# SiLU's tables kept loaded through the first projection, norms two blocks behind, and left-hand buffers 32 bytes lower

## The chip, the cores and the metric

The kernel runs on one core of one Trainium2 chip. The metric is device time in microseconds of one execution, lower is better; the times shown are medians of several runs. TensorE (PE) multiplies, with its weight loads shown as PEld; VectorE (DVE), ScalarE (ACT) and GpSimd (POOL) do the elementwise work and the gathers; SyncE (SP) issues most transfers.

## What is computed

One inference step of a one-layer encoder on 1024 prompt frames and 32 sample frames of width 1024. The part that matters here is the projection of the normalised input and the short convolution behind it:

```python
h = rms_norm(x, norm_mix_w)
proj = h @ w_in
gq, gk, gv, glr, gg, dqkv, da, db, dz = _split_cols(proj, IN_SIZES)
conv = conv_in[:, 0:l] * gdn_conv_w[0]
for i in range(1, CONV_W):
    conv = conv + conv_in[:, i:i + l] * gdn_conv_w[i]
conv = jax.nn.silu(conv)
cq, ck, cv = _split_cols(conv, (GDN_QK, GDN_QK, GDN_V))
q2 = l2_norm(cq.reshape(b, l, GDN_HEADS, GDN_DK)) * (GDN_DK ** -0.5)
k2 = l2_norm(ck.reshape(b, l, GDN_HEADS, GDN_DK))
o1 = rms_norm(o1, gla_norm_w) * jax.nn.silu(gg).reshape(b, l, GLA_HEADS, GLA_DV)
o2 = rms_norm(o2, gdn_norm_w) * jax.nn.silu(dz).reshape(b, l, GDN_HEADS, GDN_DV)
```

Two recurrent mixers (GLA and gated delta, `gla` and `gdn_free`/`gdn_state`) follow, then an output projection, a retrieval over 16384 experts (PEER: keys, top 16, gathered rows of `u` and `v`), and a final norm.

## The kernel before

Tokens are tiled by 128 (tiles 0 to 7, and "S" of 32 sample frames). `project(g)` handles three groups of tiles, PROJ; group 0 is tiles 0, 1 and S. For each group it normalises and transposes the tiles into `hh` and `hl` (a high and a low part of each number, so that three matmuls make one product), then goes through three kinds of blocks of weight columns, each weight chunk `w` being loaded by SP and split into `wh` (ACT, L191) and `wl` (DVE, L192):

- one block for gates (`win_s`) and sixteen blocks `u` by channel (`win_c`): 24 matmuls of 288 columns into `pcm` (L324);
- blocks u = 4 to 15 are the convolution's: ACT copies `pcm` to `ci`, scales it into `row` (L393), DVE adds three shifted products (L395), ACT applies SiLU in place (L397), and for the first eight of them squares `row` into `sq` (L401). `norms()` then sums the squares over channels with `pn` matmuls of one column (L364), and ACT copies `pn` to `ssn` (L366). After the eighth, `frame_norms` takes Ln and Exp of `ssn`;
- six blocks `u` by token (`win_t`) into `ptm` (L419), copied or put through SiLU into `o` (L427).

ACT holds one set of function tables at a time. SiLU is in another set than Ln and Exp, while Copy, Square and the casts run under either. `mixer_tables()` (L102) loads, at its place in the program, the set that has both Ln and Exp; where an instruction's set is not loaded, the build puts a load in front of it, under the line of that instruction.

Buffers come from pools that grow from the left (const, `sl`, `rt`, `mc`, `mx`, `p1`, later `da`) or from the right of SBUF (`gs`, `sp`, `ge`, `gp`, `dn`, `gx`, `dv`). The small `const` tiles lie in front of all other left pools, so their size shifts those.

The order of each engine's instructions is made when the kernel is built: the Tile scheduler goes through the program with a model of the engines' time and takes what is ready, by the order of the code. An edit in one place thus shifts choices far behind it. Each engine executes its own list strictly in order. After project(0), the mixers of one tile at a time are woven with the later projections (up to about 0.7 ms), then come the output projection and the routing, the gathers of expert rows `ug` and `vg` by POOL with their products on DVE and PE, and the dense half over all experts for tiles 2 to 5, `activations` (matmuls into `pD`, weights `uh`/`ul` from the pool `da`, moving `hh`/`hl` from `dn`) and `dense` (matmuls into `pV`, both operands from `dv`).

Of the kernel before, what the change touches and what calls it, by code (L numbers as in the profile page):

```python
# [11 lines left out]
F32 = mybir.dt.float32  # L12
# [3 lines left out]
U16 = mybir.dt.uint16  # L16
BF16 = mybir.dt.bfloat16
AF = mybir.ActivationFunctionType
ALU = mybir.AluOpType
AX = mybir.AxisListType  # L20

P = 128
# [10 lines left out]
OFFS = [0, 16, 24, 29, 33, 36, 38, 40, 42, 43, 44, 45, 46, 47, 48, 49]  # L33
# [36 lines left out]
def bc(ap, shape):  # L70
    return ap.to_broadcast(shape)
# [3 lines left out]
def layer_kernel(ctx: ExitStack, tc: tile.TileContext, A: dict):  # L75
    nc = tc.nc
    mm = nc.tensor.matmul

    const = ctx.enter_context(tc.tile_pool(name="const", bufs=1))
# [6 lines left out]
    rt = rctx.enter_context(tc.tile_pool(name="rt", bufs=1))  # L86
# [13 lines left out]
    def mixer_tables():  # L100

        tc.keep_in_program_order(nc.scalar.preload_act_table_set("natural_log_exp_and_others"))  # L102
# [18 lines left out]
    nc.gpsimd.iota(iota128, pattern=[[1, P]], base=0, channel_multiplier=0,  # L121
                   allow_small_or_imprecise_dtypes=True)

    offs = const.tile([P, 15], F32, name="offs")
    for q in range(15):
        nc.gpsimd.memset(offs[:, q:q + 1], float(OFFS[q + 1]))
    firsts = const.tile([P, 16], U16, name="firsts")
    for q in range(16):
        nc.gpsimd.memset(firsts[:, q:q + 1], OFFS[q] * P)

    noffs = const.tile([P, 15], F32, name="noffs")
    nc.vector.tensor_scalar(noffs, offs, -1.0, 1.0, op0=ALU.mult, op1=ALU.add)

    def row_bcast(name, src, n, pool):
        t = pool.tile([P, n], F32, name=name)
# [3 lines left out]
    def ntok(t):  # L139
        return DEC if t == "S" else P  # L140
# [126 lines left out]
    def project(g):  # L267
# [4 lines left out]
        first, last = g == 0, g == len(PROJ) - 1  # L272
# [4 lines left out]
        def pbank(name):  # L277
            turn[0] += 1
            return bank(name, streams[turn[0] % len(streams)])
# [12 lines left out]
        def chunk(src):  # L292
            w = rt.tile(list(src.shape), F32, name="w", tag="wqb", bufs=4)
            nc.sync.dma_start(w, src)
            wh = p1.tile(list(src.shape), F32R, name="wh", tag="wh", bufs=WB)
            wl = p1.tile(list(src.shape), F32R, name="wl", tag="wl", bufs=WB)
            return split(wh, wl, w)
# [20 lines left out]
        def by_channel(src):  # L318
            p = pbank("pcm")
            for kh in range(2):  # L320
                w = chunk(src[kh])
                for a, b in ((w[0], hh), (w[0], hl), (w[1], hh)):
                    for k in range(4):
                        mm(p[:, :N], a[:, k], b[:, kh * 4 + k, :N], start=b is hh and a is w[0] and kh + k == 0,  # L324
                           stop=a is w[1] and kh * 4 + k == KB - 1)
            return p

        def row_tile():
            return p1.tile([P, 3 * P], F32, name="row", bufs=2)
# [27 lines left out]
        sqs = []  # L357

        def norms():
            b, sq = sqs.pop(0)  # L360
            pn = bank("pn", "rt")
            for i, t in enumerate(tiles):
                n, o = ntok(t), i * P + (3 if t == "S" else 0)
                mm(pn[:n, i:i + 1], sq[:, o:o + n], ones[:, 0:1], start=True, stop=True)  # L364
            for i0, i1, n in pieces(g):
                nc.scalar.copy(ss[:n, i0:i1, b], pn[:n, i0:i1])  # L366
            if b == 7:
                frame_norms(g, p1, ss, ib)

        for u in range(16):  # L370
            p = by_channel(A["win_c"][u])
            if len(sqs) > (0 if u < 12 else -1) and sqs:
                norms()
            if u < 4:
                row = row_tile()
                nc.scalar.activation(row[:, :N], p[:, :N], AF.Copy, scale=0.125 if u < 2 else 1.0)
                nc.sync.dma_start(d_qk[g][:, u, :], row[:, :N])
                yield None
                continue
            b = u - 4  # L380

            nf = N - DEC if sample else N
            L = N + 3 if sample else N
            ci = p1.tile([P, 3 * P + 3], F32, name="ci", bufs=1)
            nc.vector.tensor_copy(ci[:, 0:3], hist[:, b, :])
            nc.scalar.copy(ci[:, 3:3 + nf], p[:, :nf])
            nc.vector.tensor_copy(hist[:, b, :], ci[:, nf:nf + 3])
            if sample:
                nc.vector.tensor_copy(ci[:, nf + 3:nf + 6], tails[:, b, :])
                nc.scalar.copy(ci[:, nf + 6:L + 3], p[:, nf:N])  # L390
                nc.vector.tensor_copy(tails[:, b, :], ci[:, L:L + 3])
            row = row_tile()
            nc.scalar.activation(row[:, :L], ci[:, 0:L], AF.Copy, scale=cw[:, b, 0:1])  # L393
            for i in range(1, 4):
                nc.vector.scalar_tensor_tensor(row[:, :L], ci[:, i:i + L], cw[:, b, i:i + 1], row[:, :L],  # L395
                                               op0=ALU.mult, op1=ALU.add)
            nc.scalar.activation(row[:, :L], row[:, :L], AF.Silu)  # L397
            mixer_tables()
            if b < 8:
                sq = p1.tile([P, 3 * P], F32, name="sq", bufs=1)  # L400
                nc.scalar.activation(sq[:, :L], row[:, :L], AF.Square)  # L401
                sqs.append((b, sq))
            nc.sync.dma_start(d_cv[g][:, b, 0:nf], row[:, 0:nf])
            if sample:
                nc.sync.dma_start(d_cv[g][:, b, nf:], row[:, nf + 3:L])
            yield None
        for u in range(6):
            c, hf = divmod(u, 2)
            acc = [pbank("ptm") for _ in range((ni + 1) // 2)]
            ps = [acc[i // 2][:, (i % 2) * 256:(i % 2) * 256 + 256] for i in range(ni)]  # L410
            for kh in range(4):
                w = chunk(A["win_t"][u, kh])
                for ws, hs in ((w[0], (hh, hl)), (w[1], (hh,))):
                    for i, t in enumerate(tiles):
                        n = ntok(t)
                        for k in range(2):
                            for h in hs:

                                mm(ps[i][:n], h[:, kh * 2 + k, i * P:i * P + n], ws[:, k],  # L419
                                   start=kh == 0 and k == 0 and ws is w[0] and h is hh and i % 2 == 0,  # L420
                                   stop=ws is w[1] and kh * 2 + k == KB - 1, skip_group_check=True)
                yield None
            os = []
            for i, t in enumerate(tiles):
                n = ntok(t)
                o = p1.tile([P, 256], F32, name="o", bufs=OB)
                nc.scalar.activation(o[:n], ps[i][:n], AF.Silu if c else AF.Copy)  # L427
                os.append(o)
            if c:
                mixer_tables()  # L430
            for i, (t, o) in enumerate(zip(tiles, os)):
                n = ntok(t)
                if c:
                    o3 = o[:n].rearrange("p (h e) -> p h e", h=2)
                    nc.vector.tensor_tensor(o3, o3, bc(gw[:n, c - 1, None, :], [n, 2, P]), op=ALU.mult)
                nc.sync.dma_start(d_tm[g][c, i * P:i * P + n, hf * 256:(hf + 1) * 256], o[:n])
            yield None
# [755 lines left out]
    p1 = p1ctx.enter_context(tc.tile_pool(name="p1", bufs=1))  # L1193
    spctx = ExitStack()
    sp = spctx.enter_context(tc.tile_pool(name="sp", bufs=1, side="right"))
    weave(project(0))


# [35 lines left out]
    sel, picked, mixT = {}, {}, {}  # L1234
    c1, c2, c3, chose = {}, {}, {}, [None]
    gdn_pending = {}
    behind, chosen = iter(()), []
    coming = {k: project(g) for g, ks in COMING.items() for k in ks[:1]}
    for g, ks in COMING.items():
        for k in ks[1:]:  # L1240
# [121 lines left out]
```

## Time and profile before

| | us |
|---|---|
| median of 3 runs (3272.29 to 3275.75) | 3274.96 |
| the profiled execution | 3281.99 |
| its span, first to last instruction | 3280.3 |
| PE busy in the span | 3064.6 (93%) |
| DVE busy | 2291.9 (70%) |
| ACT busy | 1282.0 (39%) |
| POOL busy | 1316.8 (40%) |

The page gives each engine's busy time, cuts the span into 40 slices with the granted TensorE clock of each, and follows the chain of work that ended last. Busy shares are means over stages with different limits, so the stages have to be read one by one: the first projection (to about 190 us), mixers and later projections (to about 700 us), routing and gathers (to about 1700 us), the dense half (to about 3200 us) and a short tail.

### The profile page before, as it was taken

The numbers are of one execution on the slowest core, as the hardware profiler recorded it, in microseconds if no ns is written. First come the engines' busy times: TensorE is split into PE (matmuls) and PEld (weight loads), VectorE is DVE, ScalarE is ACT, GpSimd is POOL, SyncE is SP. The second block draws the span as 40 slices with busy tenths as digits, with TensorE's granted clock in tenths as the row PEclk, the third lists the DMA queues.
The fourth block names the chain that finished last, engine by engine and source line by source line (L and its number), as shares of the span: only waits on it lengthen the run. The fifth ranks groups of instructions, "written<-read, shape, count | busy, mean of one in ns | idle before, by whom it ended". The sixth has DMA issues, their size and how long they took to land.

```text
span 3280.3 us, 49506 instructions
## 1 busy us (share of the span) xinstructions
PE 3064.6 (93%) x17739; PEld 2451.9 (75%) x17739; DVE 2291.9 (70%) x5692; ACT 1282.0 (39%) x2748; POOL 1316.8 (40%) x1181
## 2 busy tenths in 40 slices
PE   6999997799999999889789999999999999999997
PEld 6889986689878877767567777777777777776664
DVE  4457478888878989899977767766766767434332
ACT  6758434544332226787523222223222222223111
POOL 2100004433244544433355545544555555233454
PEclk9989998799999989899799999999999999999998
DMA  5532468888788889999999889889998898777988
GB/s 155 167 108 90 155 195 299 271 296 294 272 309 317 310 322 348 314 345 334 328 351 333 336 319 363 329 324 356 334 337 346 300 366 312 281 258 258 339 320 301
DMA packets 363977, 959.04 MB, mean 292 GB/s; under 512 B 35746, under 2 KB 137523, under 8 KB 359635
## 3 DMA queue, kind: packets, MB, share of 16 engines
q0 software_dynamic: 156672, 570.49, 47.5%
q1 hardware_dynamic: 141266, 351.84, 30.5%
q10 hardware_dynamic: 65792, 33.56, 3.5%
q8 instruction: 139, 2.28, 0.3%
q14 instruction: 108, 0.88, 0.1%
HBM read 893.00 MB, written 62.76 MB: 291 GB/s over the span
## 4 chain that ended last, share of the span: by engine, by line
PE 47%; DMA 1%; issue 1%; DVE 1%; POOL 0%; ACT 0%; POOLq 0%; DVEq 0%; ACTq 0%
PE pD L198 7%; PE pD L197 7%; PE pD L199 7%; PE pV L197 7%; PE pV L199 7%; PE pV L198 7%; PE pv L1139 6%; DMA vg<-v,eiT 1%; DMA ug<-u,ei 0%; POOL ug L1098 0%; DVE ug L1099 0%; DVE c L887 0%; DVE vl L192 0%; POOL ug L1133 0%; DVE xf L1052 0%
## 5 line engine op out<-in xcount | busy, mean ns | idle before, releaser
L1098 POOL DMA_INDIRECT ug<-u,ei x544 | 647.2, 1190 | 1148.8 <-DVE ug L1099 514.0
L1133 POOL DMA_INDIRECT vg<-v,eiT x488 | 582.9, 1194 | 625.8 <-PE pv L1139 453.2
L1099 DVE SCALAR_TENSOR_TENSOR ug<-ug,h 128x1024 f32<-128x1024 f32 x544 | 659.9, 1220 | 106.4 <-DMA ug<-u,ei 104.0
L197 PE MATMUL pD<-hh,uh 128*128 128x512 f32 x1024 | 408.6, 399 | 4.3 <-ACT uh L191 4.2
L198 PE MATMUL pD<-hh,ul 128*128 128x512 f32 x1024 | 408.6, 399 | 3.3 <-DVE ul L192 3.3
L199 PE MATMUL pD<-hl,uh 128*128 128x512 f32 x1024 | 407.4, 398 | 0.0
L198 PE MATMUL pV<-vh,wl 128*128 128x512 f32 x1024 | 401.4, 393 | 0.0
L199 PE MATMUL pV<-vl,wh 128*128 128x512 f32 x1024 | 400.0, 393 | 0.0
L197 PE MATMUL pV<-vh,wh 128*128 128x512 f32 x1024 | 381.5, 395 | 5.0 <-DVE acc L1039 4.3
L1039 DVE TENSOR_TENSOR acc<-acc,pV 128x512 f32<-128x512 f32 x248 | 164.0, 684 | 239.1 <-PE pV L199 213.0
L191 ACT CAST vh<-vx 128x1024 fp32r<-128x1024 f32 x128 | 129.2, 1047 | 509.9 <-PE pV L198 420.0
L991 ACT ACTIVATE w<-pD 128x512 f32<-128x512 f32 x128 | 76.5, 598 | 541.0 <-PE pD L199 482.3
L1139 PE MATMUL pv<-vg,wd 128*32 128x512 f32 x1952 | 267.6, 619 | 17.2 <-DMA vg<-v,eiT 16.4
L192 DVE TENSOR_TENSOR wl<-w,wh 128x512 fp32r<-128x512 f32 x302 | 207.3, 688 | 100.5 <-ACT wh L191 70.3
L191 ACT CAST wh<-w 128x512 fp32r<-128x512 f32 x302 | 186.0, 619 | 185.1 <-PE pcm L324 61.7
L534 PE MATMUL pq<-h2T,wqb 128*128 128x256 f32 (+2 forms) x1280 | 249.0, 348 | 3.5 <-ACT sc L556 2.0
L197 PEld LDWEIGHTS pD<-hh,uh 128*128 128x128 f32 x1024 | 193.4, 189 | 65.6 <-issue 14.1
L197 PEld LDWEIGHTS pV<-vh,wh 128*128 128x128 f32 x1024 | 192.3, 188 | 66.9 <-issue 14.2
L198 PEld LDWEIGHTS pD<-hh,ul 128*128 128x128 f32 x1024 | 193.3, 189 | 64.9 <-issue 12.2
L199 PEld LDWEIGHTS pD<-hl,uh 128*128 128x128 f32 x1024 | 193.2, 189 | 56.7 <-issue 11.7
L199 PEld LDWEIGHTS pV<-vl,wh 128*128 128x128 f32 x1024 | 192.7, 188 | 55.1 <-issue 14.3
L534 PEld LDWEIGHTS pq<-h2T,wqb 128*128 128x128 f32 x1280 | 211.2, 194 | 25.9 <-issue 3.0
(334 smaller groups left out, 5457.9 us busy)
## 6 DMA issues: line engine op xcount, KB each, us to landing
ux<-ut SPq DMA_DIRECT2D x128, 512.0 KB
vx<-v SPq DMA_DIRECT2D x128, 512.0 KB
wqb<-wq SPq DMA_DIRECT2D x80, 576.0 KB
gd<-gst ACTq DMA_DIRECT2D x16, 2048.0 KB
G<-gd SPq DMA_DIRECT2D x32, 1024.0 KB
w<-win_c SPq DMA_DIRECT2D x96, 256.0 KB
wch<-wout SPq DMA_DIRECT2D x40, 512.0 KB
w<-win_t SPq DMA_DIRECT2D x72, 256.0 KB
```

Source lines behind the costliest of these rows:

```text
L191: nc.scalar.copy(hi, x)
L192: nc.vector.tensor_tensor(lo, x, hi.bitcast(F32), op=ALU.subtract)
L197: mm(out, a[0], b[0], start=first, stop=False, **kw)
L198: mm(out, a[1], b[0], start=False, stop=False, **kw)
L199: mm(out, a[0], b[1], start=False, stop=last, **kw)
L534: mm(p[:, :N], w[:, kb, :], h2T[:, kb, :], start=(kb == 0), stop=(kb == KB - 1))
L991: nc.scalar.activation(w, pD, AF.Gelu_apprx_tanh)
L1039: nc.vector.tensor_tensor(acc[ti][:, cs], before[:, cs], p, op=ALU.add)
L1098: nc.gpsimd.indirect_dma_start(out=g, out_offset=None, in_=A["u"], in_offset=idx_of(ei[:, k:k + 1]))
L1099: nc.vector.scalar_tensor_tensor(g, g, 1.0, h2, op0=ALU.mult, op1=ALU.mult, accum_out=act[:, k:k + 1])
L1133: nc.gpsimd.indirect_dma_start(out=g, out_offset=None, in_=A["v"], in_offset=idx_of(eiT[:, tok:tok + 1]))
L1139: return mm(pv[half][c * 32:(c + 1) * 32, :], wd[:, c, :], vs[c][:, half * 512:(half + 1) * 512], start=(r == 0), stop=(r == ns - 1), tile ...
```

## The change

Four edits. (1) In the first projection `mixer_tables()` no longer follows each SiLU; it is called once, after the last block by token. (2) `norms()` there runs two blocks behind the squares as long as convolution blocks that square are being made, and the last two are taken one per block; `sq` of that projection comes from three buffers of the pool `rt` (tag `mixT`) and not from one of `p1`. (3) `noffs` is written by POOL directly, and `offs` and the DVE instruction that made `noffs` from it are gone. (4) `offs` took 64 bytes of each partition; `firsts` is allocated at twice its size, so that all left pools behind `const` start 32 bytes lower. Line numbers of the old kernel from L133 to L397 are three lower in the new one.

```diff
-    offs = const.tile([P, 15], F32, name="offs")
-    for q in range(15):
-        nc.gpsimd.memset(offs[:, q:q + 1], float(OFFS[q + 1]))
-    firsts = const.tile([P, 16], U16, name="firsts")
+    firsts = const.tile([P, 32], U16, name="firsts")[:, :16]
     for q in range(16):
         nc.gpsimd.memset(firsts[:, q:q + 1], OFFS[q] * P)
-
     noffs = const.tile([P, 15], F32, name="noffs")
-    nc.vector.tensor_scalar(noffs, offs, -1.0, 1.0, op0=ALU.mult, op1=ALU.add)
+    for q in range(15):
+        nc.gpsimd.memset(noffs[:, q:q + 1], float(1 - OFFS[q + 1]))
...
         for u in range(16):
             p = by_channel(A["win_c"][u])
-            if len(sqs) > (0 if u < 12 else -1) and sqs:
+            if len(sqs) > (1 if first and u < 12 else 0):
                 norms()
...
             nc.scalar.activation(row[:, :L], row[:, :L], AF.Silu)
-            mixer_tables()
+
+            if not first:
+                mixer_tables()
             if b < 8:
-                sq = p1.tile([P, 3 * P], F32, name="sq", bufs=1)
+                sq = (rt.tile([P, 3 * P], F32, name="sq", tag="mixT", bufs=3) if first else
+                      p1.tile([P, 3 * P], F32, name="sq", bufs=1))
...
-            if c:
+            if c and (u == 5 or not first):
                 mixer_tables()
```

What the scheduler made of it, at three places. PE, third to fifth convolution block of project(0), before (`pcm_836` is the next block by channel, `pn` the column sums of the squares `sq`):

```order
L324 MATMUL pcm_775<-hh_168,wl_797 128x288 x4
L364 MATMUL pn_690<-ones_84,sq_649 128x1 x2
L364 MATMUL pn_690<-ones_84,sq_649 32x1
L364 MATMUL pn_751<-ones_84,sq_710 128x1 x2
L364 MATMUL pn_751<-ones_84,sq_710 32x1
L364 MATMUL pn_812<-ones_84,sq_771 128x1 x2
L364 MATMUL pn_812<-ones_84,sq_771 32x1
L324 MATMUL pcm_836<-hh_168,wh_839 128x288 x4
```

and after:

```order
L321 MATMUL pcm_762<-hh_166,wl_766 128x288 x4
L321 MATMUL pcm_762<-hh_166,wh_783 128x288 x4
L321 MATMUL pcm_762<-hl_167,wh_783 128x288 x4
L361 MATMUL pn_739<-ones_84,sq_638 128x1 x2
L361 MATMUL pn_739<-ones_84,sq_638 32x1
L321 MATMUL pcm_762<-hh_166,wl_784 128x288 x4
L361 MATMUL pn_799<-ones_84,sq_698 128x1 x2
L361 MATMUL pn_799<-ones_84,sq_698 32x1
L321 MATMUL pcm_822<-hh_166,wh_825 128x288 x4
```

Three sums stood in a row with no block's matmuls between them; now each has some ahead of it, and nine groups of them stand behind the last of these. ACT over one of these blocks, before:

```order
L397 ACT_TABLE_LOAD
L397 ACTIVATE row<-row 128x291
L102 ACT_TABLE_LOAD
L386 COPY ci<-pcm 128x256
L390 COPY ci<-pcm 128x32
L401 ACTIVATE sq<-row 128x291
L393 ACTIVATE row<-ci,cw 128x291
L366 COPY ssn<-pn 128x2
L366 COPY ssn<-pn 32x1
```

and after:

```order
L394 ACTIVATE row<-row 128x291
L383 COPY ci<-pcm 128x256
L387 COPY ci<-pcm 128x32
L401 ACTIVATE sq<-row 128x291
L390 ACTIVATE row<-ci,cw 128x291
L188 CAST wh<-w 128x512 x2
L363 COPY ssn<-pn 128x2
L363 COPY ssn<-pn 32x1
```

The two loads are gone, and the two casts of the next weight chunks stand inside the block. The third place is on ACT where the first projection ends and the second begins (`ss` are the second's norms, `dec`, `G` and `kd` belong to the first tile's mixers), after the change:

```order
L302 ACT_TABLE_LOAD
L302 ACTIVATE ss_1922<-ss_1922,eps_86 128x1
L696 ACT_TABLE_LOAD
L696 ACTIVATE dec_1951<-pdd_1946 128x512
L591 ACTIVATE G_1970<-pgc_1967 128x256
L696 ACTIVATE dec_1994<-pdd_1989 32x128
L302 ACT_TABLE_LOAD
L302 ACTIVATE ss_1997<-ss_1997,eps_86 128x1
L303 ACT_TABLE_LOAD
L303 ACTIVATE ss_1922<-ss_1922 128x1
```

and before:

```order
L305 ACT_TABLE_LOAD
L305 ACTIVATE ss_1939<-ss_1939,eps_86 128x1
L305 ACTIVATE ss_2014<-ss_2014,eps_86 128x1
L619 ACT_TABLE_LOAD
L619 ACTIVATE E_2077<-E_2077 128x256
L306 ACTIVATE ss_1939<-ss_1939 128x1
```

Up to the second projection's first cast the program has 36 table loads before and 18 after: 12 for SiLU in L397, 17 in L102 and 7 others before; 4, 2 and 12 after. PE's list is the same again from its 1235th instruction to about the 2650th (the start of the third projection), and differs in small shifts from there to the end.

## Rows read from the trace of the kernel before

**Rows 1.** Stretches: PE, PEld, DVE, ACT, POOL busy, clock, DMA share, GB/s
```profile
62.00:80.00 18.00, 5.62 (x31) 5.16 (x30) 7.42 (x25) 15.47 (x30) 0.00 (x0) 0.64 0.26 69
...
500.00:1700.00 1200.00, 1064.29 (x6980) 906.84 (x6981) 1062.43 (x3464) 587.02 (x1590) 511.46 (x430) 0.92 0.89 312
1700.00:3200.00 1500.00, 1494.17 (x7098) 1094.88 (x7096) 919.35 (x1346) 383.86 (x501) 735.16 (x620) 1.00 0.87 324
```

**Rows 2.** Timeline of PE: start, length, instruction, count, idle before and who ended it
```profile
61.92 0.69 PE L324 MATMUL pcm<-hh,wl 128*128 128x288 f32 x4
66.67 0.80 PE L364 MATMUL pn<-ones,sq 128*128 128x1 f32 x6 [4.05 <-ACT sq L401]
71.64 1.20 PE L364 MATMUL pn<-ones,sq 128*128 128x1 f32 x6 [4.16 <-ACT sq L401]
77.00 1.20 PE L364 MATMUL pn<-ones,sq 128*128 128x1 f32 x6 [4.16 <-ACT sq L401]
...
79.26 1.16 PE L324 MATMUL pcm<-hl,wh 128*128 128x288 f32 x4
...
85.37 0.69 PE L324 MATMUL pcm<-hl,wh 128*128 128x288 f32 x4
85.91 0.69 PE L324 MATMUL pcm<-hh,wl 128*128 128x288 f32 x4
```

**Rows 3.** Timeline of ACT over one convolution block
```profile
67.73 1.28 ACT L397 ACT_TABLE_LOAD   x1
69.02 0.45 ACT L397 ACTIVATE row<-row 128x291 f32<-128x291 f32 x1
69.48 1.28 ACT L102 ACT_TABLE_LOAD   x1
70.78 0.37 ACT L386 COPY ci<-pcm 128x256 f32<-128x256 f32 x1
...
71.47 0.54 ACT L393 ACTIVATE row<-ci,cw 128x291 f32<-128x291 f32 x1
...
73.09 1.28 ACT L397 ACT_TABLE_LOAD   x1
```

**Rows 4.** Waits of PE, 0 to 210 us: total, times, longest
```profile
PE pn L364 <- ACT sq L401: 14.8, 7, 4.2
...
PE ptm L419 <- ACT wh L191: 5.0, 4, 2.1
```

**Rows 5.** Groups of ACT, 0 to 190 us: count, busy, mean ns, idle before
```profile
L191 ACT CAST wh<-w 128x512 fp32r<-128x512 f32 x60 | 36.8, 619 | 29.0 <-PE pcm L324 15.0 <-DMA w<-win_t 8.0 <-DMA w<-win_c 2.9
L102 ACT ACT_TABLE_LOAD x17 | 21.8, 1283 | 1.1 <-PEq L1345 0.8
L397 ACT ACT_TABLE_LOAD x12 | 15.4, 1283 | 0.2
...
L427 ACT ACT_TABLE_LOAD x5 | 6.4, 1283 | 0.1
```

**Rows 6.** Timeline of ACT where the second projection's norms stand
```profile
171.18 1.28 ACT L305 ACT_TABLE_LOAD   x1
...
174.59 0.28 ACT L306 ACTIVATE ss<-ss 128x1 f32<-128x1 f32 x2
```

**Rows 7.** Matmuls into `pD`, 1700 to 2700 us: count, length ns min/median/max
```profile
L197 PE MATMUL pD<-hh,uh x649: 387/395/797, 1701.8 to 2699.5; 128*128 128x512 f32 x163
```

**Rows 8.** Matmuls into `pV`, same stretch and columns
```profile
L197 PE MATMUL pV<-vh,wh x645: 387/389/497, 1701.1 to 2692.8; 128*128 128x512 f32 x162
```

**Rows 9.** DMA queues, 1700 to 2480 us: packets, MB, share of 16 engines
```profile
q0 software_dynamic: 48212, 175.56, 60.4%
q1 hardware_dynamic: 21966, 88.20, 30.3%
```

**Rows 10.** Waits of PE, 500 to 1700 us: total, times, longest
```profile
PE pgm L959 <- ACT gA L956: 42.6, 34, 8.0
...
PE pw L1082 <- DVE act L1106: 13.1, 1, 13.1
```

## Prediction

> **What bounds the kernel now.** I read the stretches first, then the timelines of PE and ACT where a stretch shows PE idle, then the waits. The dense half is PE's own: 1494 of 1500 us busy at full clock. From 500 to 1700 us no engine is full, PE busy 1064 and DVE 1062 of 1200 us, and they wait for each other [rows 1]. Whatever starts earlier in front of these stages therefore ends earlier, unless the order inside them gets worse. The change's own place is the first projection, where 62 to 80 us stands out: PE busy 5.62 of 18 us, ACT 15.47, granted clock 0.64 [rows 1]. PE's timeline tells why: from 62.6 to 78.2 us it runs nothing but three sums `pn`, each after a wait of 4.05 to 4.16 us for ACT's square `sq` [rows 2]. ACT's timeline gives the pace: from one load for SiLU to the next 5.36 us, and in it two table loads that hold the engine for 1.29 and 1.30 us [rows 3]. So in this stretch ACT sets the pace, nearly half of its step is table loads, and PE cannot pass because its list has three sums in a row.
>
> **What the change does, part by part.** All sums are made against the profiled execution, 3281.99 us, of which the span is 3280.3 us; the median of the runs is 3274.96 us, 7.0 us lower, and I take the differences over to it unchanged.
>
> *Table loads in the convolution blocks.* ACT loses 18 loads of the 36 up to the second projection: 18 x 1.283 = 23.1 us of its time [rows 5]. Without its two loads the step is 5.36 - 2.59 = 2.8 us; with the casts of two weight chunks, which stand outside the step shown and now inside, 2.8 + 2 x 0.62 = 4.0 us [rows 3, 5]. PE needs for a block six groups of four matmuls, 0.54 us from one to the next, plus one `pn` of about 0.8 us: 4.0 us [rows 2]. So the two come out level, and PE stops being held up in long stretches but has no margin. PE's waits for `sq` are 14.8 us in 7 times [rows 4]. I take 12.8 of them as gone: with three `sq` buffers and the sums apart from each other, what waited 4.1 us now has block matmuls to run meanwhile; 2 us I leave for eight sums on level engines. Bounds: none gone, since a rearranged list could still pile up, to all 14.8.
>
> *The clock.* After those idle 15 us the next groups take 1.16 us and not 0.69: PE's matmuls run at the lower of its two levels, 1.2 GHz, until about 84 us [rows 2]. Six groups and two sums at +0.47 and +0.4 us are 3.6 us, which go with the idle time. Bounds 0 to 3.6; it goes only if the waits go.
>
> *The blocks by token.* Four waits of `ptm` for a cast `wh` cost 5.0 us [rows 4]. Two or three of them stand behind table loads, and one behind a late weight load, which nothing here moves; I take half, 2.5 us. Bounds 0 to 5.
>
> *Loads that come back.* With SiLU's set resident, Exp and Ln of the gates, of `frame_norms`, of the GLA decay and of the second projection's norms each need a load of their own: of the 18 loads after, ten are such, where before there were two. Most lie beside PE work by token. Where the first projection ends that cover runs out: the second projection's transposes wait for `ss`. Before, from the first load there to the last Exp of `ss` were 3.4 us with two loads in between [rows 6]. Now the list has four loads, the mixer's `dec`, `G` and a small `dec` (some 1.3 us of work) before the first Exp of `ss`; two more loads and that work are 2 x 1.283 + 1.3 + some semaphores = 4 to 5 us later. GLA's decay is later by the same, and PE has little else there. I take +5. Bounds +0 (PE finds work by token) to +12.8 (all ten loads, 10 x 1.283, on PE's path).
>
> The Trainium skill prices this differently: its page "ScalarE: Activation LUTs", section "What ACT_TABLE_LOAD costs", has about 1.28 us for the load and 1.38 us more for a drain at every switch, 2.66 us in all. By that the 18 loads would be 47.9 us of ACT and not 23.1. The trace shows 1.29 us from the start of a load to the start of the next ACTIVATE [rows 3], so no such drain here, and the sum goes by the rows.
>
> *`noffs`, `offs`.* One DVE instruction and no net POOL instruction goes, at a time when PE waits for the first transposes. Nothing, either way.
>
> *Addresses.* By the built program's allocations, `x`, `w`, `h2T`, `ux`, `uh`, `ul`, `G` and `vx` started at multiples of 64 bytes and now start 32 beyond one; the projections' `hh`, `hl`, `wh`, `wl` the other way; the right-hand pools stay, all 32 beyond. What I can compare in the trace: gathers land 32 beyond and take 60.4% for 175.56 MB, transfers to the left pools landed at multiples and took 30.3% for 88.20 MB, which is 0.344% per MB for both [rows 9]. So nothing for DMA. One difference is there: matmuls into `pD`, whose weights `uh`, `ul` start at multiples of 64, have a median of 395 ns, those into `pV`, whose weights start 32 beyond, 389 [rows 7, 8]. With 3072 matmuls into `pD` (128 blocks of 24), nearly all in the stretch that PE bounds, 6 ns are 18.4 us. The other side: the projections' 1224 matmuls by channel (three times 17 blocks of 24) and 1296 by token (three times 24 chunks of 18) had weights 32 beyond and now have them at multiples; at 6 ns that is +15.1. Bounds -18.4 to +15.1. I take 0, since the two kinds differ in other things too (pool, moving operand, bank), and no row varies the address alone.
>
> The skill speaks against an effect: "SBUF — State Buffer", section "Door 1: The DMA port swizzle", has lines of 16 bytes in SBUF, by which 32 bytes more or less leave every operand at the start of a line and the sum stays as it is. No row here shows such a line.
>
> *The order further on.* PE's list is the same from the 1235th to about the 2650th instruction, which carries the gain through the second projection; behind that most of DVE's and PE's instructions stand some places earlier or later. I take 0. Its price from a row: from 500 to 1700 us PE is idle 136 us, 42.6 of them waits of `pgm` for ACT in 34 places and 13.1 in one wait for DVE [rows 1, 10]; a tenth of that idle time more or less is 14 us. Bounds -14 to +14.
>
> Sum: -12.8 - 3.6 - 2.5 + 5 = -13.9 us. 3274.96 - 13.9 = 3261.
>
> **Rivals.** *The returned loads eat it:* if all ten lie on PE's path, -18.9 + 12.8 = -6.1, which gives 3269. For it speaks that four stand in a row before the second projection's norms; against it that most of the others stand where PE has matmuls by token queued. That the tables don't stay loaded at all is excluded by the list of the built program. *The dense matmuls get faster:* `pD` takes `pV`'s 389 ns, -13.9 - 18.4 = -32.3, 3243. For it speaks that the difference holds over thousands of matmuls; against it that other causes fit as well, and that the projections might pay some of it back. *Slower, by the new order:* in 500 to 1700 us DVE and PE hold each other up; if DVE's new list puts more of the gather products in front of what PE waits for, PE's idle 136 us grow. At 16% more (22 us) the gain is gone and the time is 3274.96 - 13.9 + 22 = 3283; from 13.9 us on it is no gain any more. For it speaks how many instructions moved; against it that the lists moved by a few places only, and could as well gain.
>
> **How the numbers follow.** A difference below 0.2% (6.5 us) is about what a measurement of this kernel can't tell from none. Forecast, 3261, 3251 to 3271 of its own: 0.55, of which 0.03 falls within 0.2%. Returned loads, 3269: 0.12, nearly all within 0.2%. Faster dense matmuls, 3243: 0.16. Slower by order: 0.17, of which 0.05 within 0.2%. So faster 0.52 + 0.16 = 0.68, within 0.03 + 0.12 + 0.05 = 0.20, slower 0.12. The range takes in the dense case with some gain of order, 3236, and the upper end of the order's bound short of clearly slower, 3279; about 0.05 lies below it and 0.13 above.
>
> **What would show it.** PE's timeline: no wait above 1 us of `pn` for `sq`, and a clock of 1.00 where 62 to 80 us was; the last block by channel should end some 16 us earlier. ACT: 4 loads in SiLU's line of the first projection. The second projection's first `pcm` should come some 14 us earlier. The start of the dense half should keep that lead; if it doesn't, the order did it. Median lengths into `pD` of 395 say that addresses don't matter, 389 that they do. The prediction is wrong if the waits for `sq` stay, if PE idles 10 us more at the first projection's end, or if the stretch from 500 to 1700 us changes by more than 10 us.

## The result, and the profile of the changed kernel

The changed kernel takes 3226.63 us (median of 4 runs, 3219.79 to 3227.73) against 3273.62 us of the kernel before in the same comparison: ratio 0.9854, 95% interval 0.9832 to 0.9876, a gain of 47 us. The forecast was 3261 us, a gain of 13.9, and the range ended at 3236. The profiled execution of the changed kernel took 3227.73 us (span 3226.0), close to its median; that of the kernel before lies 8 us above its own, so the two traces differ by more than the medians do.

The three stretches of [rows 1] in the changed kernel (busy us and counts of PE, PEld, DVE, ACT, POOL, then clock, DMA share, GB/s):

```profile
62.00:80.00 18.00, 16.39 (x114) 16.03 (x114) 12.46 (x36) 11.23 (x36) 0.00 (x0) 0.91 0.56 150
500.00:1700.00 1200.00, 1078.33 (x7045) 911.39 (x7044) 1070.06 (x3443) 591.85 (x1590) 516.80 (x434) 0.94 0.90 318
1700.00:3200.00 1500.00, 1498.48 (x7231) 1102.74 (x7230) 916.08 (x1342) 388.32 (x511) 757.33 (x643) 1.00 0.88 329
```

The hole between 62 and 80 us is closed: PE is busy 16.39 us where it was 5.62, at a clock of 0.91 where it was 0.64. Its timeline there (start, length, instruction, count, idle before and who ended it), which answers [rows 2]:

```profile
64.66 0.76 PE L361 MATMUL pn<-ones,sq 128*128 128x1 f32 x6 [1.61 <-ACT sq L401]
65.35 0.79 PE L321 MATMUL pcm<-hh,wh 128*128 128x288 f32 x4
...
67.48 1.16 PE L321 MATMUL pcm<-hh,wh 128*128 128x288 f32 x4
...
71.22 0.69 PE L321 MATMUL pcm<-hh,wl 128*128 128x288 f32 x4
71.75 0.39 PE L361 MATMUL pn<-ones,sq 128*128 128x1 f32 x3
```

One wait of 1.61 us is left of the three above 4 us, and matmuls by channel stand between the sums. A few groups behind it, from 66.5 to 69.4 us, take 1.16 us, the lower of TensorE's two levels (1.2 GHz), and by 71.22 us they are back at 0.69. PE's waits from 0 to 210 us (total, times, longest), against [rows 4]:

```profile
PE pdc L702 <- ACT dec L696: 2.9, 1, 2.9
PE pn L361 <- ACT sq L401: 2.0, 2, 1.6
...
PE ptm L419 <- ACT wh L188: 1.6, 2, 1.4
```

The sums wait 2.0 us instead of 14.8, the matmuls by token 1.6 instead of 5.0; 2.9 us are new, for the decay `dec` whose tables must now be loaded. First start and last start of the matmuls by token (`ptm`, first from the first projection) and of the queries (`pq`), first before, then after:

```profile
L419 PE MATMUL ptm<-wh,hh x432: 274/282/580, 104.5 to 819.8; 128*128 128x256 f32 x144
...
L534 PE MATMUL pq<-h2T,wqb x1280: 274/379/634, 430.1 to 1561.7; 128*128 128x256 f32 x109, 128*128 128x128 f32 x37, 128*128 128x160 f32 x37
```

```profile
L419 PE MATMUL ptm<-wh,hh x432: 274/282/469, 88.9 to 799.5; 128*128 128x256 f32 x144
...
L534 PE MATMUL pq<-h2T,wqb x1280: 275/379/634, 414.4 to 1531.3; 128*128 128x256 f32 x109, 128*128 128x128 f32 x37, 128*128 128x160 f32 x37
```

The lead is 15.6 us at the first `ptm` and still 15.7 at the first `pq` (14.6 and 14.3 in a second pair of profiles, e16 and e13 below). So the front gained about what was forecast, 13.9. The rest lies further on. The matmuls into `pD` and `pV` of the changed kernel, 1700 to 2700 us (count, length ns min/median/max), against [rows 7, 8]:

```profile
L194 PE MATMUL pD<-hh,uh x660: 387/389/504, 1699.7 to 2699.8; 128*128 128x512 f32 x165
```

```profile
L194 PE MATMUL pV<-vh,wh x656: 387/389/504, 1708.6 to 2698.4; 128*128 128x512 f32 x164
```

`pD` has taken `pV`'s median of 389 ns. The whole dense half, from the first matmul into `pD` to the end of the span (length, PE busy and count, clock, DMA share, GB/s), in the kernel before and in the changed one:

```profile
1603.00:3280.30 1677.30, 1644.63 (x7804) 0.99 0.87 323
```

```profile
1576.80:3226.00 1649.20, 1625.58 (x7804) 0.99 0.88 329
```

The same 7804 matmuls take 28.1 us less from first to last: 19.0 us less of PE's own time and 9.1 us less idle (32.7 to 23.6). Two causes are mixed in that, the addresses and the order, and the experiments take them apart.

### The profile page after: what moved, and what is told of

It is laid out like the page before. It is cut to its first block, busy times and chain, and to the rows that moved or that the text cites. A ratio compares the mean times of both kernels' runs of the same rounds, so it can differ in the third digit from the quotient of the medians.

```text
span 3226.0 us, 49510 instructions
## 1 busy us (share of the span) xinstructions
PE 3045.9 (94%) x17739; PEld 2448.0 (76%) x17739; DVE 2293.4 (71%) x5691; ACT 1260.6 (39%) x2732; POOL 1319.6 (41%) x1181
## 4 chain that ended last, share of the span: by engine, by line
PE 48%; DVE 1%; DMA 1%; issue 0%; ACT 0%; POOL 0%; POOLq 0%; DVEq 0%
PE pD L195 7%; PE pD L194 7%; PE pD L196 7%; PE pV L194 7%; PE pV L195 7%; PE pV L196 7%; PE pv L1139 6%; DMA vg<-v,eiT 1%; DVE ug L1099 0%; DVE vl L189 0%; DVE c L887 0%; DVE xf L1052 0%; POOL vg L1133 0%; ACT rs_junk L164 0%; DVE ul L189 0%
## 5 line engine op out<-in xcount | busy, mean ns | idle before, releaser
L194 PEld LDWEIGHTS pV<-vh,wh 128*128 128x128 f32 x1024 | 192.1, 188 | 65.6 <-issue 15.9
L195 PEld LDWEIGHTS pD<-hh,ul 128*128 128x128 f32 x1024 | 192.7, 188 | 60.4 <-issue 15.9
L194 PEld LDWEIGHTS pD<-hh,uh 128*128 128x128 f32 x1024 | 192.8, 188 | 58.4 <-issue 11.6
L196 PEld LDWEIGHTS pD<-hl,uh 128*128 128x128 f32 x1024 | 192.7, 188 | 55.9 <-issue 15.9
L195 PEld LDWEIGHTS pV<-vh,wl 128*128 128x128 f32 x1024 | 193.2, 189 | 54.5 <-issue 13.4
```

What stands on the lines that cost most here:

```text
L194: mm(out, a[0], b[0], start=first, stop=False, **kw)
L195: mm(out, a[1], b[0], start=False, stop=False, **kw)
L196: mm(out, a[0], b[1], start=False, stop=last, **kw)
```

## Experiments on the addresses

In the following, a distance is the address of `uh` (the weights of a matmul into `pD`) less that of `hh` (its moving columns), modulo 256 bytes. By the built programs it is 32 in the kernel before and 0 in the changed one; between `wh` and `vh`, the operands of `pV`, it is 0 in both. The runs e1, e3, e4 and e5 came first, under rules that the later runs replaced.

**e1_before_up32** is the kernel before with 32 unused bytes ahead of the other left buffers (distance 64):

```diff
+    const.tile([P, 8], F32, name="spare")
     ident = const.tile([P, P], F32, name="ident")
```

> The kernel before with an unused buffer of 32 bytes in front of all left pools; every instruction and its order as before, only the left buffers lie 32 bytes higher. Weights of the pD matmuls start 32 bytes beyond a multiple of 64, as their moving operand does; the projections' operands both start at multiples of 64. Theory S (a high-low matmul runs at its quick pace when both operands start at the same place modulo 64): start to start of pD goes from 0.234 to 0.227 us, the projections' stays at 0.133 and 0.176, time 3274 - 20 = 3254. Theory W (weights that start at a multiple of 64 are slow): pD quick but the projections slow, 3254 to 3269. Theory O (only the order of instructions counts): 3274 and pD at 0.234.

Measured: 3277.08 us, ratio 0.9993 [0.9972, 1.0013]. **e4_before_right32** puts the same 32 bytes ahead of the right-hand pools (`gs.tile([P, 8], ...)`), which moves `hh` down and leaves `uh` (distance 64 again).

> The kernel before with 32 unused bytes at the right end, so that all right pools lie 32 bytes lower and the left ones as before. Both operands of pD and both of pV then start at multiples of 64. Theory S: pD at 0.227, pV still at 0.227, 3254. Theory W: pD stays at 0.234 and pV goes to 0.234, 3274 + 20 = 3294. A theory that only the moving operand counts (quick or slow by its own place): pD and pV change together, 3294 or less. Theory O: 3274.

Measured: 3279.55 us, 0.9997 [0.9982, 1.0012]. Neither gained. The places modulo 64 are equal in both, so S falls as it was stated, and so does W: in e1 the weights no longer start at a multiple of 64.

**e3_after_up32** is the changed kernel with those 32 bytes put back on the left: its order, the addresses of before (distance 32).

> The changed kernel with the same unused 32 bytes, so that its left buffers lie again where they lay relative to 64 before the change; all instructions and their order as in the changed kernel. Theory S and W: pD back at 0.234 us, 3227 + 20 = 3247 (W: less what the projections then gain). Theory O: 3227. What stays of the gain against the kernel before, some 27 us, is that of the tables, norms and order.

Measured: 3255.51 us, 0.9915 [0.9890, 0.9941]: some 20 us of the gain are lost and 28 stay (12 are lost by the later comparison of the changed kernel, e13, at 0.9878), so the order alone (O) is neither all nor nothing. **e5_after_dv32** is the changed kernel with 32 unused bytes between the dense stage's `wh` and `vh`; they move `wh` down, so that here `pV` is the pair off by 32 bytes, at distance 224.

> The changed kernel with 32 unused bytes between the weights and the moving operand of the pV matmuls (pool dv), so that the weights start at a multiple of 64 and the moving operand 32 beyond one. Theory S and W: pV at 0.234 in place of 0.227 over 3072 matmuls, pD unchanged at 0.227, 3227 + 20 = 3247. Theory O: 3227.

Measured: 3254.55 us, 0.9930 [0.9908, 0.9952]: slower than the changed kernel by about as much. The same can be done to `pV` as was done to `pD`, so the pool, the bank or the place in the program need not be what makes `pD` slow. Left were rules on the distance modulo some larger step.

**e2_before_up96** puts 96 bytes on the left of the kernel before (distance 128), **e8_after_uh16** moves `uh` and `ul` of the changed kernel 16 bytes up inside longer tiles. Each of the two has two buffers, used in turn; as a row of the longer tile is no multiple of 256 bytes, the distance is 16 in one and 144 in the other:

```diff
-        uh = da.tile([P, KB, P], F32R, name="uh", bufs=2)
-        ul = da.tile([P, KB, P], F32R, name="ul", bufs=2)
+        uh, ul = [da.tile([P, KB * P + 32], F32R, name=x, bufs=2)[:, 4:KB * P + 4]
+                  .rearrange("p (k c) -> p k c", k=KB) for x in ("uh", "ul")]
```

> The kernel before, its order untouched, with an unused piece of 96 bytes ahead of the other buffers on the left, so that uh and ul begin 32 bytes past a multiple of 128 (64 before, 96 in the run with 32 bytes), as hh and hl of the same matmul do on the right; by a multiple of 256 they differ now by 128. Theory A (a matmul of this kind is quick only where its weights and its columns begin at the same place modulo 128): pD starts every 227 ns instead of 234, 3072 of them give back about 20 us, the ratio to before is about 0.994 (3258 us where before is 3277). Theory A256 (the same modulo 256): pD stays at 234 ns, ratio 0.997 to 1.002. Theory O (the order alone makes the changed kernel faster): ratio 0.998 to 1.002 with pD at 234 ns.

> The changed kernel with uh and ul moved 16 bytes up inside a longer tile each, so that they begin 48 bytes past a multiple of 128 while hh and hl begin at 32. Theory A with any difference counting: pD goes to 233 to 235 ns, and the time is about 20 us over the changed kernel's (ratio to the kernel before about 0.992, as for the changed kernel with uh 32 bytes higher, 0.9915). Theory A with a grain of 32 bytes or more: pD stays at 227 ns and the ratio at 0.985 to 0.987.

Measured: e2 3279.70 us, 0.9997 [0.9977, 1.0016]; e8 3248.73 us, 0.9902 [0.9877, 0.9926]. A multiple of 128 is not enough, and 16 and 144 bytes are too much. Then **e11_before_da480**, which moves `uh` and `ul` of the kernel before, and of the rest only `G` behind them, to a distance of 0 modulo 512, and **e10_before_up224** (224 bytes on the left, 256 modulo 512):

```diff
+        (blk or da.tile([P, 120], F32, name="spare"))
         uh = da.tile([P, KB, P], F32R, name="uh", bufs=2)
```

> The kernel before, its order and all its other addresses untouched, with an unused piece of 480 bytes ahead of uh and ul alone: the distance from uh to hh, 32 more than a multiple of 512 bytes before, becomes a multiple of 512, as it is in the changed kernel (and as between the operands of pV, which start every 227 ns in both). Theory A512 (a dense matmul is quick where the distance between its weights and its columns is a multiple of 512 bytes): pD's median spacing goes from 234 to 227 ns, its mean from 233.3 to 228.2, 3072 of them give back 15.4 us, ratio to before 0.994 to 0.997. Theory O (the order alone speeds the changed kernel, and pD's pace comes along with it or is lost again in the waits of this order): ratio 0.998 to 1.002, with pD at 234 ns, or at 227 and the time gone into waits for the gathered rows.

> The kernel before, its order untouched, with 224 unused bytes ahead of the other buffers on the left: the distance from uh to hh becomes 256 more than a multiple of 512 bytes. With 128 more it was slow (232 ns, ratio 0.9997). Theory A512: pD stays at 231 to 234 ns, ratio 0.998 to 1.002. Theory A256 (a multiple of 256 is enough): pD at 227 ns, ratio 0.994 to 0.997.

Measured: e11 3258.43 us, 0.9975 [0.9954, 0.9995]; e10 3257.66 us, 0.9970 [0.9949, 0.9992]. Both gain, on the kernel before in its own order, so a multiple of 256 suffices (A256), though e11's ratio lies just outside the 0.994 to 0.997 expected of it. PE's busy time by `pD` alone says it without the scatter of whole runs (from 1500 us to the end; all 3072 matmuls in each). First distance 0, in e11, e10 and the changed kernel:

```profile
1500.00:3290.00 1790.00, 739.43 (x3072) 0.98 0.86 318
```

```profile
1500.00:3290.00 1790.00, 740.99 (x3072) 0.98 0.86 319
```

```profile
1500.00:3290.00 1790.00, 741.47 (x3072) 0.98 0.86 317
```

and then before (32), e3 (32), e1 (64), e2 (128) and e8 (16 and 144 in turn):

```profile
1500.00:3290.00 1790.00, 757.36 (x3072) 0.98 0.87 322
```

```profile
1500.00:3290.00 1790.00, 757.08 (x3072) 0.99 0.87 321
```

```profile
1500.00:3290.00 1790.00, 756.65 (x3072) 0.98 0.87 321
```

```profile
1500.00:3290.00 1790.00, 753.00 (x3072) 0.98 0.88 324
```

```profile
1500.00:3290.00 1790.00, 755.06 (x3072) 0.99 0.87 321
```

Two groups, 739 to 744 and 753 to 758 us in all the profiles, whatever the order; from before to the changed kernel 757.36 - 741.47 = 15.9 us. In e5 the same measure for `pV` is

```profile
1500.00:3290.00 1790.00, 752.07 (x3072) 0.99 0.87 319
```

against 740.08 in the changed kernel. Is it the distance, or the place of one operand? In e4 `wh` lies at the same addresses as in e5, and `vh` 32 bytes lower than there, which leaves `pV` at distance 0:

```profile
1500.00:3290.00 1790.00, 741.05 (x3072) 0.98 0.87 321
```

So the weights' place alone does not decide, and nor does that of the columns, as `vh` lies at the same addresses in e5 and in the changed kernel. The dense half of e11, from its first matmul into `pD`, is

```profile
1581.10:3241.50 1660.40, 1625.58 (x7804) 0.99 0.88 327
```

against 1677.3 us in the kernel before (1673.0 in a second profile of it, below), so nearly all of the pace stays there: 14.8 us from the mean of the two. In e10 it is 1665.0 us (from 1585.0 to 3250.0), 10.2 less; its waits for gathered rows are longer, 20.5 us against 16.4 in the kernel before. The whole runs say 13 to 14 us by the medians and 8 to 10 by the ratios, whose intervals run from 2 to 15 and from 3 to 17. **e12_after_p1_384** asks whether the projections' own matmuls, at distance 128 in both kernels, would gain too; 384 unused bytes between `hl` and `wh` of `p1` make it 0.

> The changed kernel, its order untouched, with 384 unused bytes between hh, hl and wh, wl of the projections, whose distance (128 more than a multiple of 512 bytes in the kernel before and after) becomes a multiple of 512. Theory P (the projections' matmuls pcm and ptm obey the same rule as pD): pcm of 384 columns, which start every 175 to 176 ns, come down by 3 to 5 ns, and ptm (118 to 119 ns) by 2 to 4, some 2400 of them 7 to 11 us together, of which 3 to 9 reach the end: ratio 0.001 to 0.003 under that of the changed kernel in the same call. Theory Q (shorter matmuls don't care, or are quick already): spacings as they were, the same ratio as the changed kernel within 0.002.

Measured: 3231.15 us, 0.9874 [0.9840, 0.9908], beside 0.9878 for the changed kernel in the same comparison. PE's time by `pcm` falls from 238.55 to 236.32 us, that by `ptm` rises from 173.23 to 174.75: theory Q, nothing that counts.

## Experiments on the order

**e6_tables_only** takes one part of the change into the kernel before, **e7_norms_only** the other; addresses stay.

```diff
 # e6
-            mixer_tables()
+            if not first:
+                mixer_tables()
...
-            if c:
+            if c and (u == 5 or not first):
                 mixer_tables()
 # e7
-                sq = p1.tile([P, 3 * P], F32, name="sq", bufs=1)
+                sq = (rt.tile([P, 3 * P], F32, name="sq", tag="mixT", bufs=3) if first else
+                      p1.tile([P, 3 * P], F32, name="sq", bufs=1))
-                if len(sqs) > (0 if u < 12 else -1) and sqs:
+                if len(sqs) > (1 if first and u < 12 else 0):
```

> The kernel before with one part of the change: in the first projection the tables for SiLU stay loaded (no loads of the other tables between the blocks); norms stay one block behind, addresses stay as before. Theory T (ACT's table loads are what the norms wait for): the pn waits of 14.8 us in the first 210 us fall to under 4, the granted clock in 62 to 80 us is 0.9 or more, the first ptm begins 10 to 16 us earlier (104.5 us before, 88.9 in the changed kernel), and the ratio to before is 0.990 to 0.996, pD staying at 234 ns. Theory N (that the norm is asked for too early is what costs, whatever ACT does between): the first ptm begins 0 to 5 us earlier, ratio 0.998 to 1.002.

> The kernel before with the other part of the change: in the first projection the norms come two blocks behind (with the squares in the buffers of the mixer's outputs), the table loads stay, addresses of uh, ul, hh and hl stay as before. Theory T: ACT's loads still stand in the way of each block's SiLU, the first ptm begins 0 to 5 us earlier, ratio 0.998 to 1.002. Theory N: the pn waits are gone, and the first ptm begins 10 to 16 us earlier, ratio 0.990 to 0.996. Both theories right in part (either edit takes most of the wait away): 10 us or more in this run and in the run with the tables alone, so that the two gains add up to more than the 15.6 us of the whole.

Measured: e6 3258.30 us, 0.9938 [0.9914, 0.9961]; e7 3259.68 us, 0.9942 [0.9919, 0.9964]. The waits of the sums, 14.8 us before and 2.0 after, are in e6

```profile
PE pn L364 <- ACT sq L402: 4.5, 3, 2.5
```

and in e7

```profile
PE pn L364 <- ACT sq L402: 10.2, 6, 4.2
```

The loads are the larger cause of the waits and the norms the smaller; the first `ptm` comes 8.8 us earlier in e6 and 5.4 in e7, together 14.2 of the 15.6. That is nearer to T than to N, but e6 falls short of what T wanted (4.5 us of waits and not under 4, a lead of 8.8 and not 10 to 16, a clock of 0.81 and not 0.9 from 62 to 80 us): for the whole lead both edits are needed. The times are another matter. Each kernel gains some 20 us, as T had it for e6 and N for e7, but not for their reasons: the first `pq` stands at 430.9 and 429.7 us where it stood at 430.1 before. Their gain does not come out of the first projection's lead, which is lost by then. Each has an order of its own in all later stages. In e7, whose profile lies at its median, PE idles 198.9 us of the whole span, against 215.7 and 213.1 in two profiles of the kernel before, so the gain is mostly idle time and not pace; in which stage it lies was not found (the profiled run of e6, 3274.7 us, was the slowest of its six), and it stays open.

What the changed kernel's order does in the dense half can be read with equal addresses, from e3 against the kernel before. e3's dense half, and that of the kernel before in a second profile (**e16_before_again**, the kernel before unchanged):

```profile
1602.40:3263.80 1661.40, 1639.41 (x7804) 0.99 0.88 326
```

```profile
1594.30:3267.30 1673.00, 1641.23 (x7804) 0.99 0.87 324
```

> The kernel before itself, for the scatter of the comparison and for a second profile of it on the chip of the two late starts. Both theories: ratio 0.998 to 1.002. From the first pD to the end it takes 1672 to 1678 us, as in all five profiles of this order with uh off by no multiple of 256, wherever the first pD itself begins (1598 to 1615 us in those); the order of the changed kernel takes 1660 to 1662 there with the same distances.

Measured for e16: 3267.57 us, 0.9987 [0.9971, 1.0003], so the comparison scatters by about a tenth of a per cent. Against the mean of the two profiles of before, 1675.2 us, e3 takes 13.8 us less, of which 10.3 is idle time (22.0 against 32.7 and 31.8). PE's waits there, in the kernel before and in e3:

```profile
PE pv L1139 <- DMA vg<-v,eiT: 11.6, 5, 5.3
PE pv L1139 <- DMA ug<-v,eiT: 4.8, 1, 4.8
PE pV L197 <- DVE acc L1039: 4.3, 1, 4.3
...
PE pD L198 <- DVE ul L192: 3.3, 3, 1.2
```

```profile
PE pv L1139 <- DMA vg<-v,eiT: 6.4, 2, 5.9
...
PE pV L194 <- ACT wh L188: 3.6, 2, 2.1
PE pe L1082 <- DVE c L1063: 2.2, 1, 2.2
PE pV L194 <- DVE acc L1039: 1.6, 2, 1.4
PE pD L195 <- DVE ul L189: 0.2, 1, 0.2
```

10.0 us of the waits for gathered rows, 2.7 for `acc` and 3.1 for `ul` are gone, and 5.1 for `wh` (0.7 before) and `pe` have come. It is not one lucky profile: the dense half takes 1672.9 to 1677.3 us in six profiles of before's order at slow distances, and 1660.3 us in e8, the other profile of the changed order with `uh` at a slow distance. Which moved instruction makes the rows arrive in time was not tried.

## Does a lead of the first projection last?

The starts of the first matmul into `pD` scatter: 1594 to 1615 us in the profiles of before's order at the slow distances, 1581.1 and 1585.0 in the two at the quick ones (e11, e10), 1576.8 to 1602.4 in those of the changed order. At the last `pcm` of `hh` and `wh` the orders are still apart (670.4 to 683.7 us in before's, 644.6 to 651.2 in the changed one), but at the first `pD` the traces alone can't tell whether 15 us won at 100 us are still there. Two kernels put in a lag of known size, before and after, each in its own order: DVE gets 20 unneeded reductions ahead of its work, and 256 unused bytes on the left leave the distances alone.

```diff
+    late = nc.alloc_sbuf_tensor("late", [P, 64], F32).ap()
+    ready = nc.alloc_semaphore("ready")
+    nc.vector.memset(late[:, :32], 0.0).then_inc(ready, 1)
+    nc.vector.wait_ge(ready, 1)
+    for k in range(20):
+        nc.vector.tensor_reduce(late[:, 32 + k:33 + k],
+                                late[:, None, :32].to_broadcast([P, 32, 32]), axis=AX.XY, op=ALU.add)
     with tile.TileContext(nc, schedule_with_timeline_sim=True) as tc:
```

> The changed kernel, its order untouched, with 20 unneeded reductions (32 by 32 elements each, about 1.1 us apiece by the durations of like rows) on DVE ahead of all its other work, and 256 unused bytes on the left of SBUF, which leave all distances modulo 256 as they were: DVE, and through it PE, enters the first projection D us later (D read from the first matmul, 12 to 18 us), while the queues of the DMAs and ACT are free from the start. Theory K (a lead won in the first projection is kept to the end): by the second projection and at the first pD the lag is still near D, and the time is D over that of the changed kernel (0.9878 of before in the call with both), ratio about 0.9925. Theory L (such a lead is swallowed between 500 and 1600 us, where gathered rows come at 290 to 350 GB/s, and the gain of the order comes from the dense half alone): the first pD begins within 4 us of the changed kernel's, ratio 0.987 to 0.989.

> The kernel before with the same late start of DVE. Theory K: D us over the kernel before, ratio 1.004 to 1.0055. Theory L: ratio 0.9985 to 1.0015.

> The changed kernel once more, as the yardstick on the chip of the other runs: 0.983 to 0.988 of the kernel before. If what the dense half shows is all there is, its time lies 12 to 18 us under that of the same order with uh 32 bytes higher (ratio 0.9915).

The lag in front, from the first and last start of `pcm` in e14, where the changed kernel's first is at 18.3 us:

```profile
L321 PE MATMUL pcm<-hh,wh x408: 290/337/689, 34.6 to 663.2; 128*128 128x384 f32 x90, 128*128 128x288 f32 x46
```

D is 16.3 us (16.4 in e15, 34.7 against 18.3). At the first `pq` the lag is 17.6 us in e14 (432.0 against 414.4) and 18.4 in e15 (448.5 against 430.1). Measured: e15 3289.07 us against 3271.52 of before, 1.0047 [1.0026, 1.0068], 17.5 us later by the medians; e14 3250.05 us, 0.9935 [0.9909, 0.9961]; the changed kernel once more, e13, from an earlier comparison, 3228.36 us, 0.9878 [0.9848, 0.9907]. From 0.9878 to 0.9935 are 18.6 us; e13 itself lies 12 us under e3's ratio, the lower end of what was expected of the addresses. Theory K holds in both orders, and L, which wanted 0.987 to 0.989 and 0.9985 to 1.0015, falls: what is lost in front reaches the end, whole within the scatter of some 8 us of each ratio. A lag was tried and not a lead, and with the order behind it unchanged; where the order was dealt again, in e6 and e7, the lead of 8.8 and 5.4 us was gone by the first `pq`.

## Why the prediction came out wrong

The gain is three parts of nearly equal size: 15.6 us of lead from the first projection, 13.8 us that the order saves in the dense half (e3 against before) and 13.9 us that the addresses save there (the changed kernel's two profiles, 1649.2 and 1645.9 us, against e3's 1661.4). Together 43 us; measured were 47 in the first comparison, and in the second 43 by the medians, 40 by the ratio. The first two together, 29 us, agree with e3 as a whole (28 us, by its interval 19 to 36). The forecast held the first part and put the other two at zero.

*Waits of `pn`, 12.8 us:* right, 14.8 went to 2.0. One wait of 1.61 us is left, where the prediction named 1 us as the most. *Clock, 3.6 us:* right in kind, a little less, since 62 to 80 us came to 0.91 and not 1.00; of the 15.6 us at the first `ptm` the waits make 12.8, which leaves 2.8. *`ptm`, 2.5 us:* 5.0 went to 1.6, so 3.4. *Returned loads, +5 us:* about twice too much, and not where it was looked for. A wait of 2.9 us for `dec` came, but the second projection's first group by channel, forecast 14 us earlier, stands 18.2 us earlier; up to there the loads lie beside other work of PE. From there to the first `pq` the lead falls to 15.7, by 2.5 us; whether the loads do that was not tried. Before and after:

```profile
190.00 0.98 PE L324 MATMUL pcm<-hh,wh 128*128 128x384 f32 x4 [0.25 <-DVE hl L192]
```

```profile
171.85 1.65 PE L321 MATMUL pcm<-hh,wh 128*128 128x384 f32 x4
```

*The front as a whole:* forecast 13.9, found 15.6. ACT's loads in the first projection's line are the 4 forecast:

```profile
L394 ACT ACT_TABLE_LOAD x4 | 5.1, 1283 | 0.1
```

*Addresses, 0 of -18.4 to +15.1:* this is the step that failed first. The row for it was on the table, 395 ns against 389, and its price of 18.4 us is near the 15.9 that `pD` lost. Two things went wrong. I looked at the place of the weights alone and so set a loss in the projections against it, where what counts is the distance between a matmul's two operands; and I gave the rival 0.16 where a difference that holds over thousands of matmuls of one shape deserved more. The Trainium skill, page "SBUF — State Buffer", section "Door 1: The DMA port swizzle", has lines of 16 bytes in SBUF. What the prediction drew from it, that 32 bytes leave the sum as it is, is not borne out: 757.08 against 741.47 us in the same order.

*The order further on, 0 of -14 to +14:* the second failure, at the end of its bounds, and in another place than the one priced. From 500 to 1700 us the waits of `pgm` and `pw`, against [rows 10], fell to 35.9 and 11.6 us (38.8 and 11.6 in e13, against 45.0 and 13.8 in e16). PE's idle time there fell by 14 us, from 135.7 to 121.7, more than the 10 us that the prediction named as a sign against it, but by 7 in the second pair of profiles, and e3, with the same order, has 141.6; so no gain of the order is shown there. It is shown in the dense half, which I had called full because 1494 of 1500 us were busy [rows 1]. Its ends lie outside that window: with them, PE idled 32.7 us there. The rival that this order would cost 22 us is not seen.

The range missed for the same reason: its lower end allowed for the addresses with little of the order's gain, and both came whole.

## What to carry to other kernels

Before tuning the order around a row of like matmuls, compare their lengths with another row of the same shape; if one is some ns longer, shift one operand's buffer until weights and columns lie a multiple of 256 bytes apart, which cost 32 bytes here; this is shown for matmuls in fp32r with 512 columns, and the projections' shorter ones gained nothing. A stage that looks full over its middle should be read from its first to its last instruction, since its idle time can stand at the ends. A change to one stage re-deals the order of all later ones under a scheduler, so its own gain has to be separated from theirs by a kernel with equal order or by a lag of known size. Two halves of this change gained some 20 us each by such an order, with no lead of their own left.

## What the runs showed of the chip

A matmul of 128 by 128 weights in fp32r with 512 columns has a median of 389 ns and not 393 to 396 where weights and columns start a multiple of 256 bytes apart: 3072 of them keep PE busy 738 to 744 us and not 752 to 758, `pD` and `pV` taken together. Distances of 16, 32, 64, 128, 144 and 224 bytes, all that were tried, are on the slow side, with little between them; the shorter matmuls of the projections, taken from a distance of 128 to 0, changed by 2 us in 240 (e12). The Trainium skill, page "SBUF — State Buffer", section "A bandwidth-pool intuition that's wrong (but worth ruling out)", gives the weights a read port of their own. From that one might expect that the distance does not matter; the runs show that it does, not why.
